# A hybrid encoder block: seven half products instead of eight in both down stages, and the residuals' place

## The chip, the cores and the metric

The kernel runs on one core of a Trainium2 chip. Its time is the device time of one execution in microseconds; the median of three runs is 3343.01 us (3342.64 to 3346.67). One more execution was recorded by the hardware profiler, on which every reading below rests.

The engines are TensorE (PE, with its weight loads as PEld), VectorE (DVE), ScalarE (ACT), GpSimd (POOL) and the queue engine SyncE (SP). Transfers are issued from the queues of SP, ACT and POOL.

## The reference

The input x is 2048 x 1024 in float32, and so is the output. One layer computes

```python
h = rms_norm(x, pre_mix_g)
proj = h @ w_in                              # 1024 -> attention q, k, v; RWKV columns; two gates
y_a = chunk_band_attention(q, k, v, rel_bias)
y_b = rwkv7_time_mix(p_rwkv, ...)
merged = gate_a * (y_a @ proj_a) + gate_b * (y_b @ proj_b)
x = x + rms_norm(merged @ w_out, post_mix_g)         # the residual
hf = rms_norm(x, pre_ffn_g)
u = jnp.square(jax.nn.relu(hf @ w_up)) @ w_down      # 1024 -> 4096 -> 1024
x = x + rms_norm(u, post_ffn_g)
```

The change is about the last four lines: the residual with the second norm, the up product, the squared ReLU and the down product.

## The kernel before

The 2048 tokens are four groups of 512 (`G`), each of four tiles of 128 tokens. The **mixing** goes over the groups: RWKV, attention (`phase_attention`), then the merge (`phase_merge`), which ends with the product by w_out. Its result o (128 tokens x 1024 a tile) leaves PSUM by copies on ACT. Behind the mixing the **feed-forward** part goes over two halves of 1024 tokens (groups 0 and 1, groups 2 and 3), each an up stage (`phase_up`) and a down stage.

Every float32 product is made of three: each operand is split into a rounded high part and the rest (`split`: a cast on ACT, a subtraction on DVE), and `mm3` sums high x high, high x low and low x high. One matmul takes 128 x 128 weights and 512 columns.

The **residual** of a tile (`residual_steps`) has three steps: load o and x, square and sum on ACT, a reciprocal root on POOL, two DVE operations, x1 stored; square and sum again, root, a DVE operation; eight transposes on PE in two banks (`ps_ht`), two copies on ACT (`hf`) and two stores to `ht`, the transposed input of the up stage. Group 0's residual is in group 1's merge and group 1's in group 2's, between the w_out matmuls (`after`). Those of groups 2 and 3 are in the first down stage (`beside`), with o stored to `od` and loaded again.

The **up stage** works on pairs of blocks of 128 hidden columns, 16 pairs, by the scheme of seven half-size products instead of eight. It needs sums and differences of the two token groups' inputs, which `combinations` makes from `ht` (four loads, four subtractions, one store to `td` for each of four column blocks); they are loaded as T operands and split at the beginning. Meanwhile the stage computes eight early pairs of products (`early`) that need only the first group's input, b1 (`first_half`). An up product is 12 matmuls into one of two banks `d`; one of each pair leaves by a copy to z on ACT, the other by an addition on DVE (`hidden`), followed by ReLU on ACT and the square.

The **down stage** of half 0 (`phase_down`) is plain: 32 hidden blocks, in pairs, by eight token tiles and two column halves, added to u on DVE. That of half 1 (`phase_down_sums`) uses seven half products on twelve of the sixteen block pairs, in three batches of four pairs; two pairs ahead and two behind are plain. For it the second up stage (`sums`) also stores sums and differences of the hidden values to `sd` (`differences`: four DVE additions and four stores from POOL for each of twelve pairs). The seven products' results are added into the output quarters after the last batch, tile by tile in the output loop (L1434), ahead of the last plain blocks' addition, the norm and the store (`final`).

The kernel is written as one program; the Tile framework then orders the instructions on each engine by its own rules (those written earlier go first where they are ready). Engines run their queues in order, and a tile's buffer comes free when its last reader is done.

## Time and profile before

| | us |
|---|---|
| median of three runs | 3343.01 |
| the profiled execution | 3342.12 |
| its span | 3340.3 |
| PE busy | 3247.1 (97%) |
| DVE busy | 2282.6 (68%) |
| ACT busy | 1462.3 (44%) |
| POOL busy | 391.8 (12%) |
| up stage, half 0 (from 2034.3) | 306.0 |
| down stage, half 0 (from 2340.3) | 362.2 |
| up stage, half 1 (from 2702.5) | 308.6 |
| down stage, half 1, to its last matmul (from 3011.1) | 316.6 |
| behind the last matmul | 12.6 |

The stages are cut at the first matmul of each in the timeline of PE; five matmuls of the second up stage stand before its cut. A view of the timeline gives start, duration, engine, line, operation, tiles, count, and in brackets how long the engine sat idle before it and what released it. A view of groups gives busy time and the mean of one in ns.

### The profile page before, as it was taken

The numbers are of one execution on the slowest core, as the hardware profiler recorded it, in microseconds if no ns is written. First come the engines' busy times: TensorE is split into PE (matmuls) and PEld (weight loads), VectorE is DVE, ScalarE is ACT, GpSimd is POOL, SyncE is SP. The second block draws the span as 40 slices with busy tenths as digits, with TensorE's granted clock in tenths as the row PEclk, the third lists the DMA queues.
The fourth block names the chain that finished last, engine by engine and source line by source line (L and its number), as shares of the span: only waits on it lengthen the run. The fifth ranks groups of instructions, "written<-read, shape, count | busy, mean of one in ns | idle before, by whom it ended". The sixth has DMA issues, their size and how long they took to land. (4 is left out here: it accounts for less than half of the span.)

```text
span 3340.3 us, 49351 instructions
## 1 busy us (share of the span) xinstructions
PE 3247.1 (97%) x19089; PEld 2609.9 (78%) x19089; DVE 2282.6 (68%) x3806; ACT 1462.3 (44%) x2331; POOL 391.8 (12%) x732
## 2 busy tenths in 40 slices
PE   7999999999999999999999999999999999999998
PEld 6777787777778777777777777888888878888886
DVE  6774656765665775565774675876877777766778
ACT  4434634445644444644434644333331254554432
POOL 2210002111012110012210000111200011100002
PEclk9999999999999999999999999999999999999999
DMA  5224243125263225354224266434756364444443
GB/s 157 80 89 146 98 145 120 61 89 188 84 239 126 67 92 174 101 209 142 80 89 146 85 225 222 133 116 140 272 172 202 108 242 170 170 165 154 152 151 126
DMA packets 164945, 478.42 MB, mean 143 GB/s; under 512 B 17436, under 2 KB 34016, under 8 KB 162024
## 3 DMA queue, kind: packets, MB, share of 16 engines
q1 hardware_dynamic: 110004, 364.07, 32.8%
q0 software_dynamic: 18688, 63.98, 5.0%
q10 hardware_dynamic: 36020, 47.23, 3.9%
q8 instruction: 151, 2.47, 0.3%
q14 instruction: 82, 0.67, 0.1%
HBM read 355.64 MB, written 122.71 MB: 143 GB/s over the span
## 5 line engine op out<-in xcount | busy, mean ns | idle before, releaser
L83 PE MATMUL psd<-hh,whi 128*128 128x512 f32 x1344 | 542.6, 404 | 2.3 <-DVE QA L835 2.3
L83 PE MATMUL psd<-hl,whi 128*128 128x512 f32 x1344 | 539.4, 401 | 0.0
L83 PE MATMUL psd<-hh,wlo 128*128 128x512 f32 x1344 | 536.8, 399 | 0.0
L74 ACT CAST whi<-wraw 128x1024 fp32r<-128x1024 f32 x232 | 243.6, 1050 | 537.3 <-PE psd L83 423.7
L83 PE MATMUL ps_dn<-fop 128*128 128x512 f32 x1920 | 440.6, 391 | 3.0 <-DVE u L1291 2.4
L75 DVE TENSOR_TENSOR wlo<-wraw,whi 128x1024 fp32r<-128x1024 f32 x232 | 283.1, 1220 | 214.4 <-ACT whi L74 192.1
L83 PEld LDWEIGHTS ps_dn<-fop 128*128 128x128 f32 x1920 | 359.9, 188 | 79.5 <-DVE u L1291 3.4
L83 PEld LDWEIGHTS psd<-hh,whi 128*128 128x128 f32 x1344 | 256.1, 191 | 57.5 <-issue 3.4
L83 PEld LDWEIGHTS psd<-hh,wlo 128*128 128x128 f32 x1344 | 255.7, 190 | 54.0 <-issue 3.5
L83 PEld LDWEIGHTS psd<-hl,whi 128*128 128x128 f32 x1344 | 255.6, 190 | 50.9 <-issue 2.1
L83 PE MATMUL ps_dn<-fop,fop 128*128 128x512 f32 x1008 | 228.6, 389 | 0.0
L83 PEld LDWEIGHTS ps_dn<-fop,fop 128*128 128x128 f32 x1008 | 189.2, 188 | 39.3
L1291 DVE TENSOR_TENSOR u<-u,ps_dn 128x512 f32<-128x512 f32 x240 | 160.7, 683 | 54.9 <-PE ps_dn L83 54.4
L895 DVE CUSTOM_DVE_ANT_0 sc<-bias,ps_s 128x640 f32<-128x640 f32 (+4 forms) x128 | 94.1, 735 | 54.9 <-PE ps_s L889 44.0
L74 ACT CAST fop<-wdraw 128x1024 fp32r<-128x1024 f32 x40 | 41.9, 1047 | 192.0 <-DVE u L1291 88.7
L900 ACT ACTIVATE sc<-sc,mn 128x640 f32<-128x640 f32 (+4 forms) x128 | 97.8, 764 | 35.4 <-DVE mn L895 30.1
L74 ACT CAST s12h<-s 128x1024 fp32r<-128x1024 f32 x32 | 33.7, 1054 | 168.9 <-PE ps_u L83 168.8
L1019 PE MATMUL ps_o<-whi,mh 128*128 128x512 f32 x256 | 102.4, 400 | 2.2 <-ACT o L1025 2.2
L1019 PE MATMUL ps_o<-wlo,mh 128*128 128x512 f32 x256 | 102.5, 400 | 0.6 <-DVE wlo L75 0.6
L83 PE MATMUL ps_p<-yh,whi 128*128 128x512 f32 x256 | 102.2, 399 | 0.4 <-DVE th L985 0.4
L83 PE MATMUL ps_p<-yh,wlo 128*128 128x512 f32 x256 | 102.0, 398 | 0.0
L1019 PE MATMUL ps_o<-whi,ml 128*128 128x512 f32 x256 | 101.7, 397 | 0.0
(378 smaller groups left out, 6750.6 us busy)
## 6 DMA issues: line engine op xcount, KB each, us to landing
wraw<-in_w_in_dram SPq DMA_DIRECT2D x168, 512.0 KB, 3.6
wraw<-in_w_up_dram SPq DMA_DIRECT2D x80, 512.0 KB, 4.6
ar<-sd SPq DMA_DIRECT2D x21, 1024.0 KB, 4.8
wdraw<-in_w_down_dram SPq DMA_DIRECT2D x40, 512.0 KB, 4.2
araw<-ad SPq DMA_DIRECT2D x40, 512.0 KB, 4.4
gd<-gate ACTq DMA_DIRECT2D x64, 256.0 KB, 2.3
wraw<-in_w_out_dram SPq DMA_DIRECT2D x32, 512.0 KB, 3.6
ad<-r POOLq DMA_DIRECT2D x64, 256.0 KB, 2.4
```

The lines of the kernel that those rows point to most:

```text
L74: self.nc.scalar.copy(hi, src)
L75: self.nc.vector.tensor_tensor(lo, src, hi.bitcast(F32), ALU.subtract)
L83: mm = nc.tensor.matmul(ps, l, r, start=start and n == 0, stop=stop and n == last).ins
L895: nc.vector.tensor_tensor_reduce(sc[:, 0:n], bias[:, s0:640], pss[:, c0 : c0 + n], 1.0, 3.0e38, ALU.add, ALU.min, mn,)
L900: nc.scalar.activation(sc[:, 0:n], sc[:, 0:n], AF.Exp, scale=-1.0, bias=mn, accum_out=sm)
L1019: nc.tensor.matmul(ps[t], l[:, k, ts], r[:, k % 2], start=k == 0 and j == 0, stop=k == KB - 1 and j == 2)
L1291: nc.vector.tensor_tensor(u[t][:, ns], u[t][:, ns], ps, ALU.add)
```

## The change

Five things are changed.

1. `phase_down` now is the scheme of seven half products for both halves, and the plain stage is gone. The first up stage makes the sums and differences too. In both, ReLU's square is on ACT (it was on DVE in the first) and the store of hidden values goes from ACT's queue (it was POOL's).
2. Group 2's residual goes into group 3's merge, between the w_out matmuls. Group 3's goes behind the w_out product, from o as it stands in SBUF, without the store to `od` and the load from it.
3. `combinations` works in half widths (eight rounds of four loads, four subtractions and a store), with loads from POOL's queue (they were SP's). For half 0 it is in group 3's attention (it was in its merge), for half 1 beside the products of the first down stage.
4. In the last batch the order of the products is 1, 5, 6, 3, 4, 7, 2, and the partial sums are joined as soon as their products are there (`joins`). The output loop works in column halves (`halve`), and stores halves from two queues (POOL's alone in the first down stage).
5. The second up stage's b1 is loaded in the first down stage behind its last operand load, into a pool of its own; some tiles' pools change place.

```diff
@@ phase_attention
+            early = self.combinations(0, pp) if g == self.NG - 1 else iter(())
             for p in range(NP):
                 self.att_pair(g, p)
+                advance(early, 2)
@@ phase_merge
             advance(between)
+            if g == self.NG - 1:
+                rp = e(tc.tile_pool(name="mgr", bufs=2, reuse_waits="tile"))
+                res = [self.residual_steps(g, rp, pt, *self.gs, t, o[t]) for t in range(GT)]
+                for i in range(GT + 2):
+                    for t in (i - 2, i - 1, i):
+                        if 0 <= t < GT:
+                            advance(res[t], 1)
@@ after
-        if 0 < g < 3:
-            gs = self.gains(sp, 3)
-            res = [self.residual_steps(g - 1, self.late, pt, *gs, t) for t in range(GT)]
+        if g > 0:
+            self.gs = self.gains(sp, 3 if g + 1 < self.NG else 2)
+            res = [self.residual_steps(g - 1, self.late, pt, *self.gs, t) for t in range(GT)]
@@ combinations
         for k in range(KH):
-            b = mp.tile([P, 4, G], F32, tag="cmb", bufs=bufs, name="cmb")
-            for i, src in enumerate((g0[:, k], g1[:, k], g0[:, KH + k], g1[:, KH + k])):
-                nc.sync.dma_start(b[:, i], src)
-            for o, x, y in ((0, 1, 0), (1, 3, 1), (3, 3, 0), (2, 2, 3)):
-                nc.vector.tensor_tensor(b[:, o], b[:, x], b[:, y], ALU.subtract)
-            nc.gpsimd.dma_start(self.td[half][:, :, k], b)
-            yield
+            for s in range(2):
+                ts = slice(s * G // 2, (s + 1) * G // 2)
+                b = mp.tile([P, 4, G // 2], F32, tag="cmb", bufs=1, name="cmb")
+                for i, src in enumerate((g0[:, k], g1[:, k], g0[:, KH + k], g1[:, KH + k])):
+                    nc.gpsimd.dma_start(b[:, i], src[:, ts])
+                for o, x, y in ((0, 1, 0), (1, 3, 1), (3, 3, 0), (2, 2, 3)):
+                    nc.vector.tensor_tensor(b[:, o], b[:, x], b[:, y], ALU.subtract)
+                nc.gpsimd.dma_start(self.td[half][:, :, k, ts], b)
+                yield
@@ phase_up, hidden
-                if not sums:
-                    nc.vector.tensor_tensor(out, out, out, ALU.mult)
-                    nc.gpsimd.dma_start(self.ad[fb][:, th], out)
-                    return
                 nc.scalar.activation(out, out, AF.Square)
@@ phase_down (was phase_down_sums)
+            def halve(th, t, n, gt, scaled, ssq):
+                ns = slice(n * H, (n + 1) * H)
+                u = y[th][:, t, ns]
+                sq = cb.tile([P, G], F32, tag="c", name="squ")
+                nc.scalar.activation(sq, u, AF.Square, accum_out=ssq[:, n : n + 1])
+                nc.vector.tensor_tensor(scaled[:, ns], u, gt[:, ns], ALU.mult)
...
-            steps = [(b, m) for b in range(BATCHES) for m in order]
+            steps = [(b, m) for b in range(BATCHES) for m in (order if b < BATCHES - 1 else (1, 5, 6, 3, 4, 7, 2))]
+            joins = {
+                6: ((xs, m1),), 3: ((c12, xs), (c12, v5)), 4: ((c11, m1),),
+                7: ((v7, xs), (c21, v7), (v5, v7), (c22, v5)),
+            }
...
                 product(b, m, *f)
+                if i % 2:
+                    advance(beside, 1)
+                if b == BATCHES - 1:
+                    for o, x in joins.get(m, ()):
+                        for t in range(GT):
+                            add(o, x, t)
...
+            if nxt_half:
+                beside = self.first_half(2 * half + 2, nxt_half(), self.loaded)
@@ run
-            def beside(op, pt):
-                for g in (2, 3):
-                    yield from self.residuals(g, op, pt)
-                yield from self.combinations(1, op)
-                yield from self.first_half(2, bp)
-
-            advance(self.first_half(0, bp))
-            self.phase_up(0, zp, rp, cb, pn, 8)
-            self.phase_down(0, zp, rp, cb, pn, beside)
-            self.phase_up(1, zp, rp, cb, pn, 8, True)
-            self.phase_down_sums(1, zp, bp, rp, cb, pn)
+            ahead = ExitStack()
+            with ExitStack() as c:
+                bp = bpool(c, "b")
+                advance(self.first_half(0, bp))
+                self.phase_up(0, zp, rp, cb, pn, 8)
+                self.phase_down(0, zp, bp, rp, cb, pn, lambda: bpool(ahead, "b1", side="right"))
+            self.phase_up(1, zp, rp, cb, pn, 8)
+            ahead.close()
+            self.phase_down(1, zp, bpool(ctx, "b2"), rp, cb, pn)
```

What this makes of the order shows best on ACT, where group 3's merge ends and the first up stage begins (o is the w_out result, z and r are the up products' results, a1h, s12h and s3h are high parts of up weights, od the store of o). Before:

```order
L1025 COPY o_18791<-ps_o 128x512
L1531 DMA od_0_331<-o_18791 128x1024
L1025 COPY o_18792<-ps_o 128x512
L1025 COPY o_18793<-ps_o 128x512
L1025 COPY o_18794<-ps_o 128x512
L1531 DMA od_1_332<-o_18792 128x1024
L1531 DMA od_2_333<-o_18793 128x1024
L1531 DMA od_3_334<-o_18794 128x1024
L1213 COPY z<-ps_u 128x512
L74 CAST a1h<-wraw 128x1024
L1190 ACTIVATE r<-r 128x512
L1213 COPY z<-ps_u 128x512
```

And in the change at the same place (sqo and sqx are the two squares of a residual, xr its x):

```order
L74 CAST s3h<-wraw 128x1024
L1026 COPY o_18884<-ps_o 128x512
L1026 COPY o_18885<-ps_o 128x512
L1026 COPY o_18886<-ps_o 128x512
L1047 ACTIVATE sqo,ssqo<-o_18883 128x1024
L1211 COPY z<-ps_u 128x512
L1055 ACTIVATE sqx_19487,ssq_19488<-xr 128x1024
L74 CAST a1h<-wraw 128x1024
L1047 ACTIVATE sqo,ssqo<-o_18884 128x1024
L1192 ACTIVATE r<-r 128x512
L1211 COPY z<-ps_u 128x512
L1065 COPY hf<-ps_ht 128x512 x2
```

The stores of o are gone, and the squares and transposed copies of group 3's residual stand between the z copies and ReLUs of the early products; the second square of a tile stands ahead of the next tile's first.

On PE, 36 matmuls into the first up stage, there was before a run of up matmuls and nothing else. In the change the first eight transposes of that residual stand here (bh and bl are the parts of b1, ident the unit matrix):

```order
L83 MATMUL ps_u<-bh,s12h 128x512
L83 MATMUL ps_u<-bl,s12h 128x512
L83 MATMUL ps_u<-bh,s12l 128x512
L1063 MATMUL ps_ht<-ident,o_18883 128x128 x8
L83 MATMUL ps_u<-bh,s12h 128x512
```

The next three sets of transposes follow after 25, 11 and 23 more up matmuls.

On DVE, at the very end, the last two tiles of the output loop had before the joins of the partial sums (v and y) among their work (rs_r is the root, x1r the residual):

```order
L1434 TENSOR_TENSOR y_26958<-y_26958,v_26962 128x512
L1434 TENSOR_TENSOR v_26961<-v_26961,v_26962 128x512
L1446 TENSOR_TENSOR y_26958<-y_26958,g_post_28787 128x1024
L1434 TENSOR_TENSOR y_26958<-y_26958,v_26961 128x512
L1449 SCALAR_TENSOR_TENSOR y_26958<-y_26958,rs_r,x1r 128x512 x2
L1377 TENSOR_TENSOR y_26958<-y_26958,ps_dn 128x512 x2
L1446 TENSOR_TENSOR y_26958<-y_26958,g_post_28787 128x1024
L1449 SCALAR_TENSOR_TENSOR y_26958<-y_26958,rs_r,x1r 128x512 x2
```

and in the change

```order
L1307 TENSOR_TENSOR y_26875<-y_26875,ps_dn 128x512
L1371 TENSOR_TENSOR scaled<-y_26875,g_post_28758 128x512
L1307 TENSOR_TENSOR y_26875<-y_26875,ps_dn 128x512
L1371 TENSOR_TENSOR scaled<-y_26875,g_post_28758 128x512
L1381 SCALAR_TENSOR_TENSOR scaled<-scaled,rs_r,x1r 128x512 x2
```

The joins have left the loop, and the scaling by the gain comes in halves, the first of them ahead of the second half's addition.

164 lines of the change are left out of this document (47 added, 117 removed).

## The prediction

> **What bounds the kernel now.** I read the page's busy shares first, then the windows cut at the stages, then the groups of the tiles that the change touches, and last the chain of waits for the end.
>
> ```profile
> span 3340.3 us, 49351 instructions
> PE 3247.1 (97%) x19089; PEld 2609.9 (78%) x19089; DVE 2282.6 (68%) x3806; ACT 1462.3 (44%) x2331; POOL 391.8 (12%) x732
> ```
>
> TensorE is busy for 97% of the span. The windows (each row: the stretch, its length, busy time of PE, PEld, DVE, ACT, POOL, then granted clock, DMA share and GB/s) are group 3's output projection, first up stage, first down stage, second up stage, second down stage to its last matmul, and the tail:
>
> ```profile
> 1986.00:2034.30 48.30, 45.86 (x191) 36.48 (x190) 23.06 (x23) 17.95 (x22) 0.71 (x1) 0.96 0.63 232
> 2034.30:2340.30 306.00, 305.04 (x1346) 252.19 (x1346) 227.32 (x313) 116.42 (x156) 33.64 (x63) 1.00 0.44 151
> 2340.30:2702.50 362.20, 359.08 (x1606) 296.54 (x1605) 288.32 (x377) 102.64 (x145) 36.16 (x73) 1.00 0.56 187
> 2702.50:3011.10 308.60, 305.32 (x1342) 251.21 (x1341) 233.46 (x315) 159.85 (x225) 30.55 (x54) 1.00 0.55 191
> 3011.10:3327.70 316.60, 316.04 (x1393) 260.80 (x1391) 240.57 (x281) 118.38 (x155) 14.44 (x20) 1.00 0.41 146
> 3327.70:3340.30 12.60, 0.00 (x0) 0.00 (x0) 5.98 (x9) 1.33 (x4) 3.03 (x5) 0.62 0.21 83
> ```
>
> In all but the last, PE leaves about 3 us or less: a matmul less is time less, a PE wait is time more. DVE is the next, at 76 to 80% in the down stages. The chain of waits gives the price of one 128x512 matmul in a full queue: 176.64/778 and 254.63/1122, both 0.227 us.
>
> ```profile
> 2834.49 176.64 PE ps_u L83 x778
> 3039.07 254.63 PE ps_dn L83 x1122
> ```
>
> **The change part by part.** *Down stage of half 0.* Before, it is 32 blocks x 8 token tiles x 2 column halves x 3 = 1536 matmuls. The scheme that half 1 already runs has 8 plain blocks (384) and 21 products of 4 x 4 x 3 (1008): 1392. The 144 fewer are 144 x 0.227 = 32.7 us. The stage also loses 64 transposes of the residuals, which go elsewhere. These cost more than their width:
>
> ```profile
> 2364.79 0.85 PE L83 MATMUL ps_dn<-fop 128*128 128x512 f32 x3
> 2366.32 1.06 PE L1054 MATMUL ps_ht<-ident,o_prev 128*128 128x128 f32 x8 [0.68 <-DVE o_prev L1048]
> 2367.14 2.09 PE L83 MATMUL ps_dn<-fop 128*128 128x512 f32 x8
> ```
>
> Eight transposes hold PE from 2366.32 to 2367.14, 0.82 us, so 6.6 us for 64. I don't add such pieces but take the twin: half 1's down stage, which runs the new code's scheme, needs 316.6 us to its last matmul; half 0's needs 362.2 less five early matmuls of the next stage (1.1), 361.1. **Term 1: 316.6 - 361.1 = -44.5 us** (32.7 + 6.6, and 5.2 of stalls that the twin doesn't have). The operand loads on SP's queue and the splits on ACT and DVE that the scheme adds are in the twin's time, hidden behind its PE.
>
> *The first up stage* now forms sums and differences like the second: 48 more additions on DVE, squares on ACT, 48 stores from POOL. The second does all that with PE at 305.32 of 308.60, so its steady part costs nothing; the cover is DVE's 24% of free time there.
>
> *Residuals of group 2* move into group 3's output projection, where groups 1 and 2 have theirs. Group 1's four:
>
> ```profile
> 977.75 1.09 PE L1054 MATMUL ps_ht<-ident,o_prev 128*128 128x128 f32 x8 [0.70 <-DVE o_prev L1048]
> 984.86 1.06 PE L1054 MATMUL ps_ht<-ident,o_prev 128*128 128x128 f32 x8 [0.88 <-DVE o_prev L1048]
> 992.79 1.06 PE L1054 MATMUL ps_ht<-ident,o_prev 128*128 128x128 f32 x8 [1.06 <-DVE o_prev L1048]
> 1000.88 1.06 PE L1054 MATMUL ps_ht<-ident,o_prev 128*128 128x128 f32 x8 [0.50 <-DVE o_prev L1048]
> ```
>
> Each waits 0.5 to 1.1 us, 0.8 on the mean, and takes 0.82. **Term 2: 4 x 1.6 = +6.5 us**; between 3.3 (no wait) and 8.
>
> *Residuals of group 3* stand between the last w_out matmul and the up stage's beginning. PE's queue has the first eight transposes behind 36 up matmuls, 36 x 0.227 = 8.2 us in, then after 25, 11 and 23 more. One residual's chain:
>
> ```profile
> 969.24 1.06 ACT L1038 ACTIVATE sqo<-o_prev 128x1024 f32<-128x1024 f32 x1 [0.59 <-DMA o_prev<-od]
> 971.65 1.28 DVE L1040 SCALAR_TENSOR_TENSOR o_prev<-o_prev,rs_p,g_post_mix 128x1024 f32<-128x1024 f32 x1 [1.75 <-POOL rs_p L133]
> 974.29 1.06 ACT L1046 ACTIVATE sqx<-xr 128x1024 f32<-128x1024 f32 x1
> 976.41 1.28 DVE L1048 SCALAR_TENSOR_TENSOR o_prev<-xr,rs_r,g_pre_ffn 128x1024 f32<-128x1024 f32 x1 [0.92 <-POOL rs_r L130]
> 2032.50 0.59 ACT L1025 COPY o<-ps_o 128x512 f32<-128x512 f32 x1 [7.79 <-PE ps_o L1019]
> ```
>
> 8.5 us from first square to transposes (977.75). The first copy of o starts 1.8 us before PE ends with w_out at 2034.3; four copies and a split, 3.4 us, stand ahead of the first square on ACT, so it starts 1.6 us after that end, so the first transposes are ready near 10.1 and PE waits 2. Behind it ACT's queue holds the up stage: z copies, Relu and Square, weight and T splits. Both product banks wait for them (z's copy frees one, DVE's addition the other), so an ACT late by more than a product (12 x 0.227 = 2.7 us) stops PE.
>
> ```profile
> L74 ACT CAST whi<-wraw 128x1024 fp32r<-128x1024 f32 x232 | 243.6, 1050 | 537.3 <-PE psd L83 423.7
> L1190 ACT ACTIVATE r<-r 128x512 f32<-128x512 f32 x86 | 54.2, 630 | 33.1 <-DVE r L1189 32.9
> L1056 ACT COPY hf<-ps_ht 128x512 f32<-128x512 f32 x32 | 17.3, 587 | 13.8 <-PE ps_ht L1054 11.2 <-DMA ht<-hf 2.3
> ```
>
> Up to the first split after the eight early products ACT has 18 wide casts x 1.05 = 18.9, 8 squares x 1.24 (1.06 and 0.18 to read the sum) = 9.9, 21 half copies x 0.59 = 12.4, 14 Relu/Square x 0.63 = 8.8: 50 us, begun 1.8 us early and with 3 us of waiting for the first xr: ready at 51. PE's own work there is 192 x 0.227 + 4 x 0.82 = 46.9. So 4 us at least by ACT's count; 3.2 by the row of group 1 (4 x 0.8). Walking both queues with these durations, every wait kept in order, I get up to 15 (four waits of 1 to 4 us at the transposes, the rest where z's copy stands behind the T casts). I take the middle, 9. **Term 3: 9 + 4 x 0.82 = +12.3 us.**
>
> A PE wait has a second price:
>
> ```profile
> 2009.28 0.39 PE L1019 MATMUL ps_o<-whi,ml 128*128 128x512 f32 x1
> 2011.44 0.50 PE L1019 MATMUL ps_o<-whi,mh 128*128 128x512 f32 x1 [1.77 <-ACT o L1025]
> 2013.21 0.62 PE L1019 MATMUL ps_o<-wlo,mh 128*128 128x512 f32 x1
> 2013.63 0.63 PE L1019 MATMUL ps_o<-whi,ml 128*128 128x512 f32 x1
> 2016.62 0.40 PE L1019 MATMUL ps_o<-whi,mh 128*128 128x512 f32 x1
> ```
>
> After a wait of 1.8 us the matmuls come 0.42 us apart instead of 0.227, from 2013.2 to 2016.6: 3.4 us at about half clock for eight matmuls, 1.6 lost. **Term 4: two such stretches in the up stage's beginning, +3.2 us**; none to four, 0 to 6.4. [...]
>
> *Combinations.* SP's loads and half-width work before:
>
> ```profile
> L1104 SPq DMA_DIRECT2D cmb<-ht x32: 319/424/543, 1944.4 to 2555.7; - x32
> L1106 DVE TENSOR_TENSOR cmb<-cmb x32: 681/685/693, 1954.0 to 2564.9; 128x512 f32<-128x512 f32 x32
> L1107 POOL DMA_DIRECT2D td<-cmb x8: 711/714/771, 1957.8 to 2565.9; - x8
> ```
>
> Now each half has 32 loads and 8 stores on POOL's queue, and 32 subtractions of half the width on DVE, an estimated 0.34 us each: 11 us, as before. One set lies beside group 3's attention, one beside the products, where the row below leaves DVE room. What stands behind a waiting subtraction on DVE is the attention's scores or a product's bank; behind a POOL store that waits, the bias masks of the attention.
>
> *The end of the last batch.* DVE's additions of the partial sums (32 of 128x512, 0.68 by the first row, 0.61 from start to start in a pair: 1.28 for two, further below) leave the output loop and go between the last products:
>
> ```profile
> L1434 DVE TENSOR_TENSOR y<-y,v x12: 681/683/686, 3271.7 to 3327.7; 128x512 f32<-128x512 f32 x12
> 3207.00:3283.70 76.70, 76.70 (x340) 63.52 (x339) 59.64 (x71) 27.26 (x28) 0.00 (x0) 1.00 0.28 96
> ```
>
> 59.6 + 32 x 0.61 = 79 us of DVE in 76.7 (a few are in the row already): full, and 16 of them fall behind one product of 10.9 us. Four product banks cover a lateness of some 8 us. **Term 5: +1 us in each down stage, +2**; 0 to 8.
>
> *The tail.* Now DVE is late at the end:
>
> ```profile
> 3330.20 1.28 DVE L1377 TENSOR_TENSOR y<-y,ps_dn 128x512 f32<-128x512 f32 x2
> 3331.63 0.61 ACT L1443 ACTIVATE squ<-y 128x512 f32<-128x512 f32 x1
> 3332.41 1.23 POOL L1444 TENSOR_TENSOR ssqu<-ssqu 128x1 f32<-128x1 f32 x1 [3.57 <-ACT squ L1443]
> 3334.59 1.42 DVE L1449 SCALAR_TENSOR_TENSOR y<-y,rs_r,x1r 128x512 f32<-128x512 f32 x2 [0.99 <-POOL rs_r L130]
> ```
>
> PE ends at 3327.7, but the last addition starts at 3330.8 (the second of the pair), because each tile has four joins ahead of it. Without them a tile costs DVE about 2 x 0.68 + 2 x 0.61 + 1.42 = 4.0 us against 24 x 0.227 = 5.4 on PE: DVE waits for PE and the last addition starts at 3327.8. That is 3.0 us; storing in halves from two queues I put at 0.6. **Term 6: -3.6 us**, between 2.5 and 4.5.
>
> *The second up stage* has 308.6 - 305.3 = 3.3 us of waits at its start. Its b operand is now loaded behind the last load of the first down stage, some 40 us of PE ahead of its use, and its T operands overlay y tiles that the output loop frees late. **Term 7: -1 us**, -3 to +1.
>
> The sum: -44.5 + 6.5 + 12.3 + 3.2 + 2 - 3.6 - 1 = **-25.1 us**. The profiled execution took 3342.1 us, 1.8 more than its span, and lies 0.9 under the median shown. 3342.1 - 25.1 = **3317 us**. All good ends give -44.5 + 3.3 + 6.5 + 0 + 0 - 4.5 - 3 = -42 (3300), all bad ones -44.5 + 8 + 18.3 + 6.4 + 8 - 2.5 + 1 = -5 (3337).
>
> **The rivals.** (a) *The beginning of the up stage hides the residual:* waits as small as group 1's (3.2 instead of 9) and no half clock: -6 - 3.2, 3308, and down to 3303 if terms 5 and 7 come out well. For it: the same scheme cost only 0.8 us each in groups 1 and 2. Against: there PE had no other use for ACT; here each product needs two evacuations within 2.7 us. (b) *DVE becomes the bound of both down stages.* With the joins (79 in 76.7) and, in half 0, 11 us of combinations, the lateness passes the four banks, 8 us in each: +14, 3331. Against: the twin kept PE full with DVE at 76%. (c) *Slower than before, through POOL's queue:* 16 rounds of four loads, four subtractions and a store share one tile, so each round waits for the store before it. If DVE's subtraction stands before a bank's release and its loads have not landed, PE stops. From 1.5 us a round (24) the gain is gone; at the 2.7 us of one product a round it is 16 x 2.7 = 43, 3360. Against it POOL issues a store in 0.54 us while DVE is 76% busy:
>
> ```profile
> L1207 POOL DMA_DIRECT2D sd<-slots x48: 539/539/631, 2792.6 to 2979.5; - x48
> ```
>
> [...] (d) *No change:* the pieces of (b) and half of (c) together with 15 us in term 3.
>
> That the half products aren't made is no rival: PE's order has 1392 matmuls in both down stages.
>
> **How the numbers follow.** Forecast, with its own range 3309 to 3326: 0.65. (a) 0.15. (b) 0.12. (c) 0.04. (d) 0.04. For 8 in 10 the range takes the forecast's, most of (a) and the lower part of (b): 3303 to 3329. About 0.2%, 6.7 us, is what a measurement of this kernel can tell from no change: faster is under 3336.3. Forecast, (a) and (b) all lie there: 0.92; same 0.04; slower 0.04.
>
> **What would show it.** Term 1: the first down stage in the windows at 316 to 320 us, with 2784 matmuls of ps_dn in all. Terms 2 to 4: ps_ht with four waits under 1 us in group 3's projection and four of 1 to 4 us in the first 40 us of the up stage, z copies of ACT as PE's releaser, and a first up stage of 319 to 325 us instead of 306; if it is under 312, (a) holds. Term 5: PE waits for DVE in the last three products. Term 6: 9 us behind the last matmul. (c) would show as DVE waiting for cmb's loads. The prediction falls if the first up stage loses over 25 us, or if a stage before group 3's attention, which I left alone, moves by more than 3.

## The result, and the profile after

The changed kernel takes 3369.89 us (median of six, 3368.72 to 3372.68) against 3344.24 us of the kernel before on the same chip (six, 3341.80 to 3346.67): a ratio of 1.0078, with a 95% interval of 1.0069 to 1.0088. It is 0.8% slower; the forecast was 3317.0 us, faster. The first rows of the page after:

```profile
span 3367.0 us, 49210 instructions
PE 3232.2 (96%) x18945; PEld 2589.7 (77%) x18945; DVE 2280.6 (68%) x3790; ACT 1554.1 (46%) x2463; POOL 422.7 (13%) x804
```

PE has the 144 matmuls less (18945 for 19089) and is busy for 14.9 us less, but the span is 26.7 us longer: idle time on PE has grown by 41.6 us. The 144 matmuls alone are 32.7 us; PE's busy time falls by less because a matmul is busy for longer at a halved clock (12 in 5.00 us at 0.52, 16 in 3.40 us at 1.00, in windows below), and the records of the granted clock, from 30 us on to the last matmul, show 82 us at half where there were 41. The windows of the stages (columns as in the prediction) are group 3's attention, its merge, first up, first down, second up, second down, tail:

```profile
1773.90:1940.40 166.50, 155.84 (x1009) 121.17 (x1005) 98.21 (x208) 84.87 (x149) 30.46 (x62) 0.99 0.50 165
1940.40:2053.40 113.00, 107.65 (x531) 85.51 (x529) 70.78 (x90) 55.02 (x82) 12.04 (x24) 1.00 0.62 214
2053.40:2382.30 328.90, 314.81 (x1377) 258.19 (x1377) 239.22 (x315) 171.56 (x247) 39.74 (x76) 0.98 0.55 188
2382.30:2708.50 326.20, 319.98 (x1392) 262.28 (x1392) 257.17 (x323) 122.22 (x157) 35.47 (x66) 0.99 0.51 178
2708.50:3033.70 325.20, 311.74 (x1346) 254.53 (x1345) 227.23 (x310) 159.03 (x226) 30.12 (x58) 0.98 0.51 175
3033.70:3357.70 324.00, 318.92 (x1393) 262.50 (x1391) 250.64 (x297) 123.73 (x160) 6.73 (x21) 0.99 0.43 150
3357.70:3367.00 9.30, 0.02 (x1) 0.00 (x0) 4.61 (x7) 1.45 (x4) 0.93 (x3) 0.69 0.31 113
```

Stage lengths in us, cut at the stages' matmuls (in the second column the forecast's terms are added to the first; e2 to e18 are experiments below):

| stage | before | forecast | after | e2 | e7 | e14 | e18 |
|---|---|---|---|---|---|---|---|
| group 3's attention | 153.9 | 153.9 | 166.5 | 154.6 | 154.2 | 154.3 | 155.5 |
| its merge | 108.4 | 114.9 | 113.0 | 113.8 | 113.2 | 113.2 | 113.0 |
| first up | 306.0 | 321.5 | 328.9 | 329.1 | 329.0 | 329.7 | 325.8 |
| first down | 362.2 | 318.7 | 326.2 | 318.0 | 318.3 | 317.7 | 317.9 |
| second up | 308.5 | 307.5 | 325.2 | 326.1 | 314.5 | 310.6 | 309.4 |
| second down | 316.3 | 317.3 | 323.6 | 323.0 | 323.3 | 322.5 | 322.5 |
| tail | 13.0 | 9.4 | 9.7 | 9.7 | 9.9 | 8.1 | 8.1 |

The gain of the products is there. It is given back in four places.

**Attention, +12.6.** DVE waits for the loads of the combinations (releaser, total, times, longest; attention alone), which before it never did there:

```profile
DVE cmb L1109 <- DMA cmb<-ht: 16.4, 10, 3.7
```

One such wait in the timelines of POOL, DVE and PE:

```profile
1882.83 2.18 POOL L1107 DMA_DIRECT2D cmb<-ht  x4 [5.17 <-issue]
...
1885.89 0.43 DVE L1109 TENSOR_TENSOR cmb<-cmb 128x256 f32<-128x256 f32 x1 [2.57 <-DMA cmb<-ht]
...
1889.16 0.42 DVE L1109 TENSOR_TENSOR cmb<-cmb 128x256 f32<-128x256 f32 x1 [2.04 <-DMA cmb<-ht]
1889.50 0.55 DVE L903 TENSOR_SCALAR sc<-sc,rs 128x640 f32<-128x640 f32 x1
...
1890.19 1.30 PE L907 MATMUL ps_pt<-ident,sc 128*128 128x128 f32 x5 [4.00 <-DVE sc L903]
```

POOL issues the four loads from 1882.83 to 1885.01. The subtractions stand at the head of DVE's queue at 1883.32 and at 1887.12, before their pieces have landed; the scaling of the scores (L903) is behind them, and PE's transposes behind that.

**First up stage, +22.9.** PE's waits in the stage:

```profile
PE ps_ht L1063 <- DVE o L1057: 5.9, 3, 3.5
PE ps_u L83 <- ACT z L1211: 4.4, 1, 4.4
PE ps_u L83 <- DVE s12l L75: 1.6, 1, 1.6
PE ps_u L83 <- ACT s12h L74: 1.0, 1, 1.0
PE ps_u L83 <- DVE s3l L75: 0.8, 2, 0.5
PE ps_u L83 <- ACT s3h L74: 0.3, 1, 0.3
```

14.0 us, where the stage before had only the 1.0 for s12h. The first row is the residual's transposes. For the second, ACT's timeline:

```profile
2099.22 1.04 ACT L1115 CAST t3h<-t3l 128x1024 fp32r<-128x1024 f32 x1 [1.55 <-DMA t3l<-td]
2101.32 1.04 ACT L1115 CAST t1h<-t1l 128x1024 fp32r<-128x1024 f32 x1 [1.05 <-DMA t1l<-td]
2102.27 0.58 ACT L1211 COPY z<-ps_u 128x512 f32<-128x512 f32 x1
```

z's copy stands behind casts that wait for their loads.

**Second up stage, +16.7.** Rows of PE, ACT and DVE at its start:

```profile
2716.40 0.80 PE L83 MATMUL ps_u<-bh,a1h 128*128 128x512 f32 x1 [7.51 <-ACT a1h L74]
2719.45 0.79 PE L83 MATMUL ps_u<-bh,a1l 128*128 128x512 f32 x1 [1.83 <-DVE a1l L75]
2728.78 0.50 PE L83 MATMUL ps_u<-bh,s12h 128*128 128x512 f32 x1 [2.38 <-ACT z L1211]
...
2713.39 0.63 ACT L1370 ACTIVATE squ<-y 128x512 f32<-128x512 f32 x1 [3.36 <-DVE y L1307]
2715.32 1.03 ACT L74 CAST a1h<-wraw 128x1024 fp32r<-128x1024 f32 x1
2726.25 1.04 ACT L74 CAST s3h<-wraw 128x1024 fp32r<-128x1024 f32 x1 [5.88 <-DMA out_dram<-scaled]
...
2716.65 1.41 DVE L1381 SCALAR_TENSOR_TENSOR scaled<-scaled,rs_r,x1r 128x512 f32<-128x512 f32 x2 [1.33 <-POOL rs_r L130]
2718.17 1.23 DVE L75 TENSOR_TENSOR a1l<-wraw,a1h 128x1024 fp32r<-128x1024 f32 x1
```

PE's last down matmul is at 2708.5, the output loop's last squares on ACT at 2714.7. The first weight is cast behind them, its remainder follows the loop's last scaling, and s3h waits for a store of an output row.

**Second down stage, +7.3.** One stop, 32.7 us into the stage, behind its first 120 matmuls; before, the same place cost 0.55 us:

```profile
3066.38 18.84 PE L83 MATMUL ps_dn<-fop 128*128 128x512 f32 x72 [4.03 <-DVE y L1307]
```

**The halved clock** makes most of these waits dearer. Windows behind waits of 3.37, 4.00, 4.88, 2.38 and 4.03 us, the last in two pieces:

```profile
1823.60:1827.60 4.00, 4.00 (x18) 3.31 (x19) 3.74 (x6) 0.58 (x1) 0.00 (x0) 1.00 0.90 316
1890.20:1892.20 2.00, 2.00 (x8) 1.81 (x9) 1.91 (x5) 0.67 (x1) 0.15 (x1) 0.50 0.00 0
...
2509.50:2515.50 6.00, 6.00 (x16) 4.72 (x17) 6.00 (x7) 2.94 (x3) 0.00 (x0) 0.56 0.34 142
2728.80:2732.20 3.40, 3.40 (x10) 2.73 (x11) 3.03 (x4) 3.37 (x5) 0.00 (x0) 0.65 1.03 353
3066.40:3071.40 5.00, 5.00 (x12) 4.01 (x13) 4.58 (x6) 0.00 (x0) 0.00 (x0) 0.52 0.42 177
3071.40:3074.80 3.40, 3.40 (x16) 2.79 (x15) 3.16 (x4) 0.00 (x0) 0.00 (x0) 1.00 0.00 0
```

Behind 4.88 us, PE gets through 16 matmuls in 6.0 us, which at 0.227 are 3.6: 2.4 lost. Behind 3.37 us nothing is lost; the clock stays at 1.00.

### The profile page after: what moved, and what is told of

The parts are those of the page before. It is cut to its first block, busy times and chain, and to the rows that moved or that the text cites. A ratio compares the mean times of both kernels' runs of the same rounds, so it can differ in the third digit from the quotient of the medians.

```text
span 3367.0 us, 49210 instructions
## 1 busy us (share of the span) xinstructions
PE 3232.2 (96%) x18945; PEld 2589.7 (77%) x18945; DVE 2280.6 (68%) x3790; ACT 1554.1 (46%) x2463; POOL 422.7 (13%) x804
## 5 line engine op out<-in xcount | busy, mean ns | idle before, releaser
L83 PE MATMUL ps_dn<-fop,fop 128*128 128x512 f32 x2016 | 460.7, 391 | 5.4 <-DVE y L1307 5.4
L83 PEld LDWEIGHTS ps_dn<-fop,fop 128*128 128x128 f32 x2016 | 380.1, 189 | 85.7 <-issue 5.3
L74 ACT CAST fop<-ar 128x1024 fp32r<-128x1024 f32 x84 | 87.6, 1047 | 217.7 <-PE ps_dn L83 172.1
L83 PE MATMUL ps_dn<-fop 128*128 128x512 f32 x768 | 179.2, 394 | 5.9 <-DVE y L1307 4.8
L83 PEld LDWEIGHTS ps_dn<-fop 128*128 128x128 f32 x768 | 145.1, 190 | 39.4 <-DVE y L1307 6.6
L1307 DVE TENSOR_TENSOR y<-y,ps_dn 128x512 f32<-128x512 f32 x168 | 109.8, 682 | 41.0 <-PE ps_dn L83 40.8
L75 DVE TENSOR_TENSOR fop<-ar,fop 128x1024 fp32r<-128x1024 f32 x84 | 102.3, 1220 | 30.6 <-ACT fop L74 30.6
L1205 POOL DMA_DIRECT2D sd<-slots x96 | 52.0, 542 | 500.3 <-DVE slots L1204 495.1
```

Of the source, the lines that this page charges most:

```text
L74: self.nc.scalar.copy(hi, src)
L75: self.nc.vector.tensor_tensor(lo, src, hi.bitcast(F32), ALU.subtract)
L83: mm = nc.tensor.matmul(ps, l, r, start=start and n == 0, stop=stop and n == last).ins
L1205: nc.gpsimd.dma_start(place(i, "s3" if o == "a21" else o), R[o])
L1307: nc.vector.tensor_tensor(dst, dst, ps, ALU.add)
```

## The experiments

### Is it the combinations, and what in them?

**e1_ahead.** The four loads of a round are written one step ahead of its subtractions, and the rounds are spread.

```diff
...
                     nc.gpsimd.dma_start(b[:, i], src[:, ts])
+                yield
                 for o, x, y in ((0, 1, 0), (1, 3, 1), (3, 3, 0), (2, 2, 3)):
...
                 nc.gpsimd.dma_start(self.td[half][:, :, k, ts], b)
-                yield
```

> The changed kernel, with one thing done otherwise: a round of the combinations loads its four pieces one step before it subtracts them (same single buffer, still on POOL's queue), and the rounds are spread, one at the middle and one at the end of each head pair, in place of two in a row at the end. Theory A (DVE's queue is held at its head by a subtraction whose loads were issued just ahead, and the attention's own DVE work stands behind it): DVE's waits for cmb fall from 40 us to under 5, group 3's attention goes from 166.5 back to 154 to 157 us, the first down stage from 326.4 to 320 to 325, the whole to 3350 to 3358 us. Rival B (the added DVE work and transfers themselves cost, wherever they wait): attention stays over 162 us and the whole over 3363.

3373.7 us, 1.0081 (1.0065 to 1.0096) of before; attention 170.2. DVE's waits there are the same:

```profile
DVE cmb L1113 <- DMA cmb<-ht: 15.7, 9, 3.8
```

DVE's order has the same instructions in the same places as the changed kernel's, so where the rounds are written does not decide it. It seems that the framework puts each subtraction where it reckons its loads done; that is not shown. So this run decides nothing between A and B.

**e2_sp.** The same loads from SP's queue.

```diff
-                    nc.gpsimd.dma_start(b[:, i], src[:, ts])
+                    nc.sync.dma_start(b[:, i], src[:, ts])
```

> The changed kernel with only the combinations' loads issued by SP instead of POOL (stores stay on POOL). My prediction's rival was about POOL's queue. If POOL's issue (0.55 us each) or its order is what makes the loads late, attention falls from 166.5 to under 159 us and the whole to about 3360 us. Under theory A (one buffer: a round's loads wait for the store before, then DVE waits for the loads, whoever issues) it stays within 4 us of 166.5 or gets worse, since SP's queue now waits for the buffer ahead of the bias loads.

3350.5 us, 1.0013 (1.0004 to 1.0023). Attention and first down stage:

```profile
1776.70:1931.30 154.60, 153.56 (x1008) 119.87 (x1005) 97.78 (x208) 85.06 (x149) 13.10 (x30) 1.00 0.54 177
2374.20:2692.20 318.00, 317.14 (x1393) 260.44 (x1391) 257.34 (x323) 122.23 (x157) 20.19 (x38) 1.00 0.52 183
```

Loading from SP is worth 19.4 us: attention 166.5 to 154.6, first down stage 326.2 to 318.0. The order of DVE's queue changed with it. DVE's waits for cmb in the attention fall to 4.7 us, 3 times; its first subtraction now stands four instructions later and starts at 1825.57 where it started at 1821.57. Theory A's 166.5 did not come. Whether the later place or SP's shorter issue (a median of 0.42 us a load in before, for POOL's 0.55 in after) does it is not separated.

**e3_no_sub.** Loads and stores on POOL as changed, without the subtractions.

```diff
-                for o, x, y in ((0, 1, 0), (1, 3, 1), (3, 3, 0), (2, 2, 3)):
-                    nc.vector.tensor_tensor(b[:, o], b[:, x], b[:, y], ALU.subtract)
```

> The changed kernel without the combinations' subtractions (the 64 DVE subtractions are left out, so the combined operands hold plain pieces); all their loads and stores stay, on POOL, at the same places. Theory A: with nothing on DVE that waits for the loads, attention returns to 153 to 156 us and the first down stage to 319 to 323 us; the whole 3349 to 3355 us. Rival B2 (the 80 transfers or POOL's waits collide with the attention's own loads): attention stays over 162 us.

3348.6 us, 1.0006 (0.9996 to 1.0015); attention 154.3, first down stage 317.6. The 80 transfers and POOL's own waits cost PE nothing here (the attention took 153.9 before, the first down stage 318.0 in e2). With e2 this shows it: DVE's in-order wait for pieces loaded through POOL's queue costs some 20 us. It isn't DVE's added work, which e2 keeps, nor the transfers, which e3 keeps.

### The second up stage's start

**e4_late_final.** The changed kernel; the end of each row block (a tile of 128 tokens in the output loop) is put one block later (the multiplication by the gain goes with it).

```diff
...
-                    final(th, t, fp, scaled, ssq)
+                    due.append((th, t, fp, ssq))
+                    if len(due) > 1:
+                        final(*due.pop(0))
...
```

> The changed kernel with the output loop's end of a row block (multiplication by the gain, scaling, addition, stores) put one row block later, so that DVE takes the next block's sums before it waits for POOL's reciprocal root; same work. Theory C (in the loop DVE waits 1.3 us per row block for POOL's root, falls 5 us behind TensorE, and ScalarE's first cast for the second up stage stands behind the last squares): the first product of the second up stage waits 2 to 4 us instead of 7.5, the three waits together 4 to 7 us instead of 11.7, the second up stage goes from 325.0 to 315 to 320 us, the whole to 3359 to 3365 us. Rival D (the casts wait for a buffer that the loop still holds): the first wait stays over 6 us and the whole over 3367.

3367.4 us, 1.0062 (1.0046 to 1.0078); the stage takes 320.8 us. PE's waits at its start:

```profile
PE ps_u L83 <- DVE a1l L75: 3.4, 1, 3.4
PE ps_u L83 <- ACT a1h L74: 3.1, 1, 3.1
PE ps_u L83 <- ACT z L1211: 1.7, 1, 1.7
```

8.2 us for 11.7: the first wait falls as C says, but a1l's grows, and the stage and the whole stay above C's range. Part of it is something else.

**e7_loop_buffers.** e2, with the four sums (m1, xs, v5, v7) in a pool that closes behind the joins, and the output loop's buffers there instead of on the right side, on the second up stage's weights (`a1l`, `s12h`, `s3h`).

```diff
+            fs = qctx.enter_context(tc.tile_pool(name="fds", bufs=1, reuse_waits="tile"))
+            m1, xs, v5, v7 = (fs.tile([P, GT, H], F32, name=n) for n in ("m1", "xs", "v5", "v7"))
...
-            fp = e(tc.tile_pool(name="fdt", bufs=2, side="right", reuse_waits="tile"))
+            fp = e(tc.tile_pool(name="fdt", bufs=2, reuse_waits="tile"))
```

> The kernel with the combinations' loads on SP, and beside that one thing: the output loop's buffers (gain, scaled, residual rows) take the place of the four sums that the joins have used up, instead of a place that the second up stage's first weights need. Rival D of the run with the late end (the first weights' casts and remainders wait for buffers of the output loop: a1l for its small root tiles, s3h for a store of an output row): the three waits at the second up stage's start, 11.7 us, fall under 3 us, the stage goes from 326.1 to 310 to 314 us, the whole to 3334 to 3340 us. Theory C alone (DVE's 5 us lag behind TensorE in the loop): the first wait stays 4 us or more and the stage over 318 us.

3340.3 us, 0.998 (0.9971 to 0.999): 10.1 us off e2, and below the kernel before. The stage falls from 326.1 to 314.5, with two waits left:

```profile
PE ps_u L83 <- ACT z L1211: 3.7, 1, 3.7
PE ps_u L83 <- ACT s12h L74: 0.9, 1, 0.9
```

The 3.7 is a copy behind the loop's last squares. **e14_late_buffers** adds e4's edit, with e10's:

> The combinations' loads on SP, the output loop's buffers on the used sums, t1 and b22 exchanged, and the output loop's end of a row block one row block later (as in e4_late_final). Theory C and rival D both hold, one for each wait: with the buffers free, what is left at the second up stage's start is the copy of z behind the last squares (3.7 us and the halved clock behind it); with DVE in step with TensorE it goes. The second up stage falls from 315 to 309 to 312 us and the whole to 3331 to 3336 us. If it stays at 314 or more, DVE's lag is not what holds the copy.

3334.5 us, 0.9968 (0.9955 to 0.998). The stage is at 310.6 and z's wait is gone. So both hold: DVE, which in the changed kernel waits 1.3 us a row block for POOL's root (1.33, 1.32 and 1.33 in the last three), is 5 us behind PE at the loop's end (its last addition starts at 2713.91, PE's last matmul ends at 2708.89), and the buffers hold the weights.

### The second down stage's start

**e6_fetch.** e2, with ar in a pool of its own, so that the weight quarters' buffers come to lie on b1.

```diff
...
-                ar = qp.tile([P, XB, G], F32, tag="ar", bufs=2, name="ar")
+                ar = arp.tile([P, XB, G], F32, tag="ar", name="ar")
```

> The kernel with the combinations' loads on SP, and beside that one thing: in the down stages the two hidden-side buffers (ar) lie in a pool of their own, below the four weight-quarter buffers, which so come to lie on the second up stage's first-half operand instead of its last weights. Theory G (the last down stage's quarter loads wait for the very end of the up stage before it, because their buffers lie on weights that its last product reads; the first sums come late, DVE works off a backlog and TensorE stops 4.0 us): the quarter loads go out 10 us or more before the stage begins, the stop at its start goes, the last down stage falls from 323.0 to 316 to 319 us, the whole to 3343 to 3347 us. Rival H (the other order of the last batch and the joins in it cost the 7 us): the stage stays over 321 us.

3349.5 us, 1.0013 (1.0003 to 1.0022). The quarters' loads go out 13.5 us before the stage, and the stop stays:

```profile
3002.84 2.52 SPq L1325 DMA_DIRECT2D qb<-in_w_down_dram  x4
```

```profile
3048.79 18.20 PE L83 MATMUL ps_dn<-fop 128*128 128x512 f32 x72 [3.89 <-DVE y L1308]
```

G falls.

**e9_b2.** e7, with b2 on the right side, on b1.

```diff
-            self.phase_down(1, zp, bpool(ctx, "b2"), rp, cb, pn)
+            self.phase_down(1, zp, bpool(ctx, "b2", side="right"), rp, cb, pn)
```

> The kernel with the combinations' loads on SP and the output loop's buffers on the used sums (3340.3 us; first up stage 329.0, second 314.5, last down stage 323.3), and beside that one thing: the last down stage's operand buffers (b2) take the place of the second up stage's first-half operand, whose last reader is 14 us before that stage's end, and no longer the place of t4 and b22, which its very last products read. Theory I (the stage's second and third weight blocks cannot be split before the up stage has ended; DVE then has their remainders and the first operands' before it, and the sums come late: TensorE stops 4 us): the stop falls under 1 us, the last down stage goes from 323.3 to 316 to 319 us, the whole to 3332 to 3337 us. Rival H (the other order of the last batch and the joins in it): the stage stays over 321 us and the whole over 3338.

3340.2 us, 0.9985 (0.9975 to 0.9994). The stop goes (PE's waits for DVE's sums are 0.8 us in the stage), yet it takes 324.8 us: each matmul is slower (the half products' median is 398 ns). **e16_late_b2** shows the same beside e14.

> e14_late_buffers with b2 on the second up stage's first-half operand, as in e9_b2. If removing the stop at the last down stage's start is worth what it shows (4.0 us and 3.4 us of halved clock), this is 4 to 7 us below e14_late_buffers; in e9_b2 the stop went but the matmuls of that stage ran 0.6 to 2% slower each, and if that belongs to the place of the buffers, it is 0 to 3 us below or above.

3333.0 us, 0.9965 (0.9953 to 0.9978). The half products of a stretch of the stage in e16, then of the stage in e18, where b2 is on the left (min, median, max in ns):

```profile
L83 PE MATMUL ps_dn<-fop,fop x345: 397/397/398, 3119.7 to 3200.0; 128*128 128x512 f32 x173
```

```profile
L83 PE MATMUL ps_dn<-fop,fop x972: 389/389/389, 3049.8 to 3269.9; 128*128 128x512 f32 x195
```

That takes back what the stop had cost. How much it is can be worked out. From start to start, waits and half clock left out, the stage's 1392 matmuls stand 0.2327 us apart on the mean in e9 and e16, 0.2294 in e10 (below; b2 is on the right there too, and the stage takes 320.0 us), and 0.2268 in e18; in the 100 us from 3100 on PE gets through 430, 431, 439 and 443. The slower pace makes an estimated 8.2 us in e9 and e16 and 3.6 in e10. Without it their stages would take 316.6, 316.3 and 316.3 us, and before it was 316.3: by this estimate the stop, with the clock behind it, is the whole of the stage's 7 us.

**e15_old_batch.** e2, with the last batch's old order and the joins in the output loop, in the last down stage alone.

```diff
-            ... (order if b < BATCHES - 1 else (1, 5, 6, 3, 4, 7, 2))]
+            ... (order if b < BATCHES - 1 or not nxt_half else (1, 5, 6, 3, 4, 7, 2))]
-                if b == BATCHES - 1:
+                if b == BATCHES - 1 and nxt_half:
```

> The kernel with the combinations' loads on SP, and in the last down stage alone the last batch's old order of products and the joins of the sums in the output loop, as before the change. Rival H (my prediction's fifth term: joins beside the last products make DVE late): the last down stage falls from 323.0 to 316 to 318 us and the tail rises from 9.7 to 13. Otherwise (the stop at the stage's start, 4.0 us, and the halved clock behind it, 3.4 us, are the whole of the 7 us): the stage stays at 322 to 324 us and only the tail rises.

3356.3 us, 1.0035 (1.0026 to 1.0045). The stage is at 323.4, the stop again 4.0; only the tail rises, to 16.6. H falls: the order and the joins cost nothing.

**e17_t_by_half.** e14 with t2 and t3 lowest in the second up stage, so that b2 takes over their buffers.

```diff
-                for n in ("t4", "t1", "t2", "t3", "b22")
+                for n in (("t2", "t3", "t1", "b22", "t4") if half else ("t4", "t1", "t2", "t3", "b22"))
```

> e14_late_buffers (3334.5 us; last down stage 322.5), and beside that one thing: in the second up stage the full products' operands lie in another order, t2 and t3 lowest, so that b2, which stays at its old place, takes over buffers whose last readers are three to four products (8 to 11 us) before the up stage's end, not those of its last product. Theory I: the stop of 4.0 us at the last down stage's start falls under 1 us, the halved clock behind it goes, and with b2's place unchanged the matmuls keep 389 ns: the stage falls from 322.5 to 315 to 318 us, the whole to 3327 to 3331 us. If the matmuls slow down as with b2 on the right, the cause is not its place; if the stop stays, it is not the buffers.

3332.1 us, 0.9953 (0.994 to 0.9967). The last down stage takes 324.1 us. The stop stays at 4.0 us, but DVE's first remainder of a hidden block also still starts behind the stage's beginning (3001.09, 1.0 us in), where in e16 it started 12.4 us before (2986.09): the edit did not bring the splits forward, so it doesn't test I. The matmuls keep 389 ns.

### The first up stage

**e5_res_behind.** e2, with group 3's residual ranked behind the early products.

```diff
-                            advance(res[t], 1)
+                            with tc.high_priority(offset=-400):
+                                advance(res[t], 1)
```

> The kernel with the combinations' loads on SP (3350.5 us; first up stage 329.1, second 326.1, last down stage 323.0), and beside that one thing: group 3's residual steps keep their instructions but rank behind the first up stage's early products, so that TensorE's 32 transposes stand after the 192 early matmul groups' products and not among the first of them. Theory E (TensorE's queue is held by transposes that wait for DVE's rows, 5.9 us, and the halved clock behind each wait): the first up stage goes from 329 to 312 to 320 us, the whole to 3335 to 3342 us. Rival F (DVE itself, which waits for POOL's root in every row block, 3.5 us a row block, holds the early products' operands, wherever the transposes stand): the stage stays over 324 us and the whole over 3345.

3368.0 us, 1.0062 (1.0047 to 1.0077); the stage takes 346.2 us. In the early products PE now waits 3.5 us in all. But the 32 transposes come in one burst behind them, and the full products' operands after that:

```profile
PE ps_u L83 <- ACT t2h L1116: 12.1, 1, 12.1
```

**e8_all** joins e5's edit to e6's and e7's.

> All four together: the combinations' loads on SP, the residual behind the early products, the quarter buffers on the first-half operand, the output loop's buffers on the used sums. If the causes are the four named and independent, the gains add: 3350.5 less 9 to 15, less 4 to 7, less 10 to 16, so 3313 to 3328 us, which is below the kernel before the change by 0.5 to 0.9%. If one of the first three fails, it is over 3328.

3356.3 us, 1.0031 (1.002 to 1.0042): e5's loss (first up 345.0) takes back e7's gain.

**e10_t_swap** (e9, t1 and b22 exchanged), **e11_res_80** and **e12_res_120** (e10, the residual ranked 80 and 120 places later):

> The kernel of e9_b2, and beside that one thing: in the up stages the buffers of t1 and b22 change places. In the first up stage t1 lay on the buffers of group 3's residual (its rows and transposed pieces), so its load waited for the last store of it and SP's queue with it; now b22, which is needed one product later, lies there, and t1 on the gains. If that wait at the start of the full products is what costs (3.4 to 5 us of TensorE's time near 2095 us), the first up stage goes from 329 to 322 to 326 us; if the loads wait only for SP's earlier entries (the weights), it stays within 1.5 us of 329.

> The kernel of e10_t_swap, and beside that one thing: group 3's residual steps rank 80 places later, so that its first 16 transposes stand one by one among the products and the others 8 to 26 products later than before; the last still within the early products (by some 40 of the 192). Theory E for the early products, as in the run with the residual behind all of them, where TensorE's waits in them fell to 3.5 us and the cost came after: the first up stage falls by 5 to 10 us against e10_t_swap. Rival F (DVE's waits for POOL's roots hold everything): within 3 us of it, either way.

> As e11_res_80 with 120 places: the first transposes after 61 products, the last at some 130. If the loads of the full products' operands behind the residual are what costs (as in the run with the residual behind all early products, +17 us), this is 2 to 8 us slower than e11_res_80; if only the early products' waits count, 0 to 5 us faster.

3337.0 us (0.9978, 0.9968 to 0.9987), 3338.0 (0.9974, 0.9964 to 0.9984), 3344.2 (0.9995, 0.9986 to 1.0005); first up 329.7, 327.8, 333.2. With t1 and b22 exchanged the stage is where it was (329.0 in e7, 331.6 in e9), so that place isn't what costs. No rank gives the 5 to 10 us expected, and 120 is worse than 80.

**e13_no_chain.** e2 without the residual's arithmetic in group 3.

```diff
+        last = g == self.NG - 1
+        if not last:
             nc.scalar.activation(sq, o, AF.Square, accum_out=ssq)
             r = self.rstd(mp, ssq, 0.25 / D, RMS_EPS, post=0.5)
...
```

> The kernel with the combinations' loads on SP (3350.5 us; merge 113.8, first up stage 329.1), and group 3's residual without its arithmetic: the two squares, the roots, the scalings and the addition of its four row blocks are left out, so the rows go unnormalised; the row loads, the 32 transposes, the copies and all stores stay. If the chain costs (TensorE's transposes wait 5.9 us for DVE's rows, z 4 to 5 us behind, and the halved clock after each): the first up stage falls from 329 to 312 to 317 us, that is to within 4.3 us of transposes and about 3 us of 306. If the late operand loads (t2 to t4 behind the residual's buffers on SP's queue) cost by themselves: it stays over 320 us.

3343.7 us, 0.9999 (0.999 to 1.0008). First up 318.5, merge 117.5, which now has some of the transposes: 436.0 together for e2's 442.9. That lies between the two readings expected. The chain is worth 7 us of the 28.5 that the two stages had lost in e2; the rest stays with the transposes, copies and operand loads that this kernel keeps, and is not divided further.

**e18_casts_behind.** e17 with those operands' loads and casts ranked 60 later, so that ACT's order has z's copy ahead of t1's casts.

```diff
-                advance(ops, 1 + i % 2)
+                with tc.high_priority(offset=-60):
+                    advance(ops, 1 + i % 2)
```

> e17_t_by_half, and beside that one thing: the loads and casts of the full products' operands rank 60 places later, so that in ScalarE's order the copy of z stands ahead of t1's first cast and not behind it. If the casts that wait for their loads hold that copy (4.4 us and the halved clock behind it), the first up stage falls from 329 to 321 to 326 us and the whole to 3321 to 3328 us; if the products then wait for the operands themselves, it stays within 2 us of 329.

3330.5 us, 0.9952 (0.9939 to 0.9964), the lowest median here, though its runs overlap with e17's; first up 325.8. This is one trace, and stages with the same code lie up to 3 us apart (first up 328.9 to 331.6 in after, e2, e4, e6, e7, e9 and e15), but none of them is this short. The copy's wait is smaller:

```profile
PE ps_u L83 <- ACT z L1211: 2.6, 1, 2.6
```

## Why the prediction was wrong, point by point

The forecast was missed by 53 us. By the table of stages some 20 of them lie with the combinations (attention and first down stage), 18 with term 7, 7 with terms 3 and 4 in the first up stage, and 6 with term 5 in the second down stage.

*Term 1* (-44.5) is right in itself: with most of DVE's waits for cmb gone (e2, 7.0 us for 40.2 in the whole kernel) the first down stage takes 318.0 us, 44.2 less. In the changed kernel it is 36.0 less.

*Combinations, costed at nothing.* This is the step that failed most: +20 us. I counted DVE's room (11 us of work), not where an in-order queue stands when a piece is late. The mechanism was the rival (c), to which I gave 0.04, and not with its size: 20 us over 16 rounds is about 1.25 us a round, under the 1.5 from which it decides alone. Against it I set POOL's even issue; that row was right and did not bear on it. The 64 loads were issued in 0.546 to 0.596 us each: it was the wait on DVE's side. The trace of before already had that wait, five times; PE waited 0.36 us behind one of them (at 2546). The prediction does not use the row:

```profile
DVE cmb L1106 <- DMA cmb<-ht: 10.2, 5, 3.6
```

The half-width subtractions took 0.42 us each for the 0.34 estimated.

*Terms 2 to 4* (+22.0 together; term 2's 4 x 1.6 is 6.4 and not 6.5) measured +27.5: the merge +4.6 for +6.5, the first up stage +22.9 for +15.5, still under the 25 at which I said that the prediction falls. The mechanism is the one named, transposes behind DVE and z's copy behind the T casts. Mis-sized was the waiting: 13.0 us more for the 9 that I took; with 3.3 for the transposes, 6.6 are left for the clock and the rest, for 3.2. The two stretches at half clock came (3.41 us from 2077.87, 6.83 us from 2101.77); half of PE's busy time in them is an estimated 4.5 us.

*Term 5* (+2) named the wrong place. The joins cost nothing (e15). The second down stage's +7.3 is the stop of 4.0 us in its first blocks, 0.9 for a copy on ACT, and the halved clock (12 matmuls in 5.0 us, 2.3 lost). The stop goes when the second and third blocks can be split before the stage (e9, e16: 0.8 and 0.4 us of waits left in it). With b2 there the matmuls stand further apart, so no run got the stage back to 316; 320.0 in e10 is the nearest, and only the estimate above, which takes the slower pace out, gives the 7 us to the stop and the clock behind it.

*Term 6* (-3.6) was right: -3.3.

*Term 7* (-1) failed: +16.7. I looked at the T operands over y and not at the weights over the output loop's buffers, nor at ACT's order, in which the first cast stands behind the last squares. e7 and e14 take 15.5 of it away.

*Halved clock.* Term 4 priced it where I expected waits. It then cost 1.1 to 2.4 us each time in the windows above. In the trace of the change it came behind each of the ten waits of 3.49 to 7.51 us, but only behind three of the seven of 2.38 to 3.37 us (the first 30 us left out). The records of the granted clock in the traces of before and after show what goes with it. Its 19 changes in the one and 27 in the other all lie at whole multiples of 3.413 us from the first (to within 0.01 us). Carried back to the start of the span, the first such mark stands at 2.75 us in before and at 2.57 us in after. The marks cut the time into cells, and the halving went largely with how long PE was idle within one of them. The rows are the two cells that the wait of 3.37 us (1820.20 to 1823.57) falls into, then the cell of the wait of 2.38 us (2726.40 to 2728.78) and the one behind it:

```profile
1818.47:1821.88 3.41, 1.74 (x9) 1.24 (x7) 0.31 (x1) 2.27 (x4) 0.59 (x4) 1.00 1.04 396
1821.88:1825.29 3.41, 1.72 (x8) 1.45 (x9) 3.30 (x5) 0.00 (x0) 0.00 (x0) 1.00 1.00 379
2726.41:2729.82 3.41, 1.04 (x4) 0.86 (x5) 2.49 (x3) 3.41 (x5) 0.00 (x0) 1.00 1.02 419
2729.82:2733.23 3.41, 3.41 (x10) 2.63 (x9) 3.04 (x4) 2.91 (x4) 0.00 (x0) 0.50 1.03 342
```

The longer wait falls into two cells, with 1.67 and 1.69 us of idle time, and the clock stays at 1.00; the shorter one falls into one, with 2.37 us, and the next cell is at 0.50. In these two traces, from 30 us on to the last matmul, each of the 20 cells at full clock with over 1.95 us of idle time was followed by half clock, none of the 1866 with up to 1.2, and 2 of the 15 between. A wait of 2.82 us at the same place of both kernels falls into two cells in each: in before, with 1.53 and 1.29 us, half clock followed, in after, with 1.64 and 1.18 us, it did not. So the price of a wait of 2 to 3.4 us was in these traces in part a matter of chance.

*"Prediction falls if a stage before group 3's attention moves by more than 3"*: 1.9. The attention itself, which I took as untouched, moved by 12.6. The best of the runs (e18) is 13 us over the forecast still: 4.3 in the first up stage, 5.2 in the second down stage, 1.9 in the second up stage, and 4.5 ahead of group 3's attention, where nothing was edited and the profiles differ from 1772.4 to 1776.7.

## What to carry to other kernels

Work is not free because an engine has room (DVE's wait for the combinations' loads cost some 20 us here): ask for each instruction that is added to an in-order queue what it waits for and what stands behind it, and price that wait with the halved clock that can follow (here 1.1 to 2.4 us each time). Where pools are stacked, follow each buffer that a stage's first instructions need to its last reader in the stage before. A queue for loads is chosen together with the place at which the consumer stands in its own queue.

## What the hardware showed that I had not expected

Matmuls of the second down stage took 397 ns for 389 when its operand buffers were put on the other side of the pools (in e16 the half products from 3049.7 to 3278.4 took 397 or 398 each; their median is 398 in e9 and 392 in e10), at a granted clock of 1.00. Against e14 only the place of these buffers and, with it, the time of the splits differ in e16; the cause stays open.
